# Two pieces to a step among the experts, later sparse transposes, and a branch hinted early, in a two-block model on one core

## Chip, cores and metric

The kernel runs on one core of one Trainium2 chip. The metric is the time of one execution in device microseconds, the median of several; a profiled execution gives the trace. The engines are called as the profile calls them: PE is TensorE's matmuls, PEld its weight loads, DVE VectorE, ACT ScalarE, POOL GpSimd and SP SyncE, which issues the DMAs. A "q" behind an engine's name is its sequencer. [...]

## What is computed

Everything is float32, for one sequence of 256 tokens of width 1024. A first block of two layers (neighbourhood attention and differential attention) comes first, then a second block of two layers: layer 0 mixes by native sparse attention (NSA), layer 1 by multi-head latent attention (MLA), each with a cross attention to a memory, and each is followed by a mixture of experts. That mixture is where most of the weights are: 16 experts with three matrices of 2 MB each.

```python
for i in range(DEPTH):                       # second block: NSA, then MLA
    ...
    y = jnp.concatenate([mix, xa], -1) @ w_out[i]
    x = layer_norm(DEEPNORM_ALPHA * x + y, ln_g[i, 0], ln_b[i, 0])
    f = hier_moe(x, ...)                     # 16 experts, 512 wide
    x = layer_norm(DEEPNORM_ALPHA * x + f, ln_g[i, 1], ln_b[i, 1])

# hier_moe, for the 256 tokens xs of the sequence: gate[s, e] is not zero for
# two experts of one group of four
hdn = jax.nn.silu(jnp.einsum('sd,edf->sef', xs, w_gate)) * jnp.einsum('sd,edf->sef', xs, w_up)
hdn = hdn * gate[..., None].astype(hdn.dtype)
return jnp.einsum('sef,efd->sd', hdn, w_down)
```

## The kernel before

The program is one stream of about 16,000 instructions. TensorE, VectorE and ScalarE execute what stands in their queues in the order in which the kernel's text issues it; within the experts and within NSA that order is written out by hand, in steps.

**Experts.** Each expert has room for 64 tokens (CAP). The tokens of a group of four experts are gathered by products with one-hot matrices `Dg` (`gather`, line 2025, 128 x 128 tiles), and the results are brought back by products with the transposed matrices `dT` (`combine`, line 2265). `back` (line 2051) makes `dT` and the gates. Between these, expert `e` has its own products, with tiles 64 columns wide, two of which run at once in the two halves of the array: gate and up (line 2173, tile `eg`), then down (line 2213, tile `dn`), which needs the hidden values: ScalarE's activation of the gate half (line 2180), VectorE's product (2183, 2193) and its transpose (2201, tile `hT`). The last expert's down products are done in quarters of the columns (line 2241), each followed by its sums (line 2514).

The function `moe` numbers the steps, 16 per expert, one pair of products in each second. `pre[s]` and `post[s]` are lists of what is issued before and behind step `s`, filled by `at`. `piece(s, gen, delay)` runs one piece of a generator (`gather`, `back` or `combine`) behind step `s` and its evacuation from PSUM `delay` steps later. So each piece is a run of full-array matmuls between 64-column ones. The rows of the norm's gain (`ln_row`, line 922) and the sums' first products (`begin` and `add`, lines 2465 and 2470) stand in the same lists.

**Weights.** `Weights` issues 192 DMAs of 512 KB per layer on SP's queue, in the order of use, into a ring of 12 slots "w" and into the tiles "b8" and "b4" that the rest of the kernel also uses. Which slots others need, and from which step to which, stands in the table `others`; a load is issued when a slot is free by it, and starts when the tile's last readers have finished.

**Overflow.** After the experts the count of tokens of the fullest expert is loaded into a register of each engine (line 2534). A conditional block (2535) computes what did not fit into 64 places, in a loop over the experts. With these inputs no expert has more than 64 tokens, so every engine jumps over the block. The last quarter's sums (line 2514) stand behind it.

**NSA.** Six pairs of heads go through a chain of steps: scores for two key halves (line 462), maxima (361), exponentials (370), normalisation on VectorE (1418, 1419 and 164, tile `z`), transposes of the second half for each head of the pair (1426) and of the first (1437), and the products with the values (1453, 1456). Pairs start four steps apart; between them TensorE has projections of NSA's other parts (line 253), whose weights VectorE and ScalarE split into two parts (lines 134 and 135).

## Time and profile before

| | us |
|---|---|
| median of 3 runs | 1029.16 |
| lowest, highest | 1028.06, 1031.38 |
| the profiled execution | 1031.01 |
| its span in the trace, first to last instruction | 1029.2 |
| PE busy in it | 992.5 (96%) |
| DVE busy | 658.8 (64%) |
| PEld busy | 647.2 (63%) |
| ACT busy | 440.0 (43%) |
| mean granted clock | 0.987 |

In that execution NSA's sparse attention stands at about 345 to 420, the experts of layer 0 from 461 to 680, MLA from 680 to 800 and the experts of layer 1 from 800 to 1020; a few us of norm and output end it. A busy share is a mean over stages that have different limits, so the prediction goes by stretches. Matmuls are pipelined: the duration of one in a row is longer than the distance to the next, and what a run of them costs is read from start to start.

### The profile page before, as it was taken

The page shows a single profiled execution, that of the slowest core. Times are in us where ns is not written, and L with a number is a line of the kernel's source. Part 1 is how long each engine was busy: PE and PEld are TensorE (multiplying, and loading weights), DVE is VectorE, ACT ScalarE, POOL GpSimd, SP SyncE. Part 2 cuts the span into 40 slices and gives each one's busy share as a digit, 9 for nine tenths or more (in the row PEclk, how much of TensorE's full clock was granted, in tenths as well). Part 3 has the DMA queues.
Part 4 walks back from the last instruction along what each step waited for, and adds up shares of the span by engine and source line. Part 5 has one row for each costly group of instructions (what it writes and reads, how often), then busy time and mean ns, then how long its engine had stood idle before and what let it go on. Part 6 is the DMA issues. An engine that isn't in the chain of part 4 may idle for free. (4 is left out here: it accounts for less than half of the span.)

```text
span 1029.2 us, 16197 instructions
## 1 busy us (share of the span) xinstructions
PE 992.5 (96%) x5673; PEld 647.2 (63%) x5673; DVE 658.8 (64%) x1852; ACT 440.0 (43%) x1094; POOL 19.0 (2%) x38
## 2 busy tenths in 40 slices
PE   8999999999999988999999999989999999999994
PEld 8898889978897766774333433368877443434332
DVE  6767876568877777748475545548885646454556
ACT  6556664556663567543212121134883321212121
POOL 1000000000100000000000000000000000000000
PEclk9999999999999999999999999989999999999998
DMA  8954665444666623889999999982698799999994
GB/s 298 374 152 144 203 197 184 144 127 119 184 197 214 174 87 121 292 344 327 355 409 409 409 409 409 393 309 87 206 349 320 256 332 410 375 409 409 409 406 149
DMA packets 110699, 285.64 MB, mean 278 GB/s; under 512 B 14160, under 2 KB 30864, under 8 KB 110352
## 3 DMA queue, kind: packets, MB, share of 16 engines
q1 hardware_dynamic: 110608, 284.50, 76.6%
q8 instruction: 49, 0.80, 0.3%
q14 instruction: 42, 0.34, 0.1%
HBM read 283.41 MB, written 1.05 MB: 276 GB/s over the span
## 5 line engine op out<-in xcount | busy, mean ns | idle before, releaser
L135 DVE TENSOR_TENSOR wsp<-w,wsp 128x512 fp32r<-128x512 f32 (+4 forms) x272 | 170.9, 643 | 66.3 <-ACT wsp L134 64.9
L2173 PE MATMUL eg<-wa,xg 128*64 128x512 f32 x776 | 208.7, 600 | 0.0
L253 PE MATMUL pj<-xTh,wsp 128*128 128x256 f32 x768 | 154.4, 291 | 1.1 <-ACT wsp L134 0.6
L134 ACT CAST wsp<-w 128x512 fp32r<-128x512 f32 (+4 forms) x272 | 148.5, 582 | 9.3 <-PE pj L253 8.7
L253 PEld LDWEIGHTS pj<-xTh,wsp 128*128 128x128 f32 x768 | 124.0, 192 | 8.1 <-issue 4.6
L2173 PEld LDWEIGHTS eg<-wa,xg 128*64 128x64 f32 x776 | 56.3, 136 | 89.2 <-issue 83.2
L253 PE MATMUL pj<-xTl,wsp 128*128 128x256 f32 x384 | 108.8, 283 | 0.0
L253 PE MATMUL pj<-wsp,xTh 128*128 128x512 f32 (+3 forms) x352 | 108.5, 389 | 0.0
L2183 DVE SCALAR_TENSOR_TENSOR z<-z,eg 64x512 f32<-64x512 f32 x32 | 21.7, 679 | 127.0 <-ACT z L2180 127.0
L2193 DVE SCALAR_TENSOR_TENSOR hq<-z,gall,eg 32x128 f32<-32x128 f32 x256 | 88.9, 347 | 4.4
L2213 PE MATMUL dn<-wa,hT 128*64 128x512 f32 x380 | 90.4, 592 | 0.0
L2173 PE MATMUL eg<-w,xg 128*64 128x512 f32 x248 | 83.5, 600 | 0.0
L253 PE MATMUL pj<-wsp,yTh 128*128 128x512 f32 x256 | 82.8, 404 | 0.0
L2180 ACT ACTIVATE z<-eg 64x512 f32<-64x512 f32 x32 | 18.9, 590 | 144.9 <-PE eg L2173 144.9
L2223 ACT CAST ys<-dn 64x512 fp32r<-64x512 f32 x60 | 34.8, 579 | 94.5 <-PE dn L2213 63.1
L253 PEld LDWEIGHTS pj<-xTl,wsp 128*128 128x128 f32 x384 | 73.7, 192 | 0.4
L253 PEld LDWEIGHTS pj<-wsp,xTh 128*128 128x128 f32 x352 | 62.8, 188 | 11.6 <-issue 2.5
L253 PE MATMUL pj<-wsp,xTl 128*128 128x512 f32 (+3 forms) x176 | 66.7, 379 | 0.0
L2213 PEld LDWEIGHTS dn<-wa,hT 128*64 128x64 f32 x380 | 27.3, 137 | 54.3 <-issue 51.4
L370 ACT ACTIVATE z<-z,mx 128x256 f32<-128x256 f32 (+1 forms) x104 | 48.1, 468 | 12.9 <-DVE mx L361 12.9
L253 PEld LDWEIGHTS pj<-wsp,yTh 128*128 128x128 f32 x256 | 45.8, 188 | 9.9 <-issue 1.9
L253 PE MATMUL pj<-wsp,yTl 128*128 128x512 f32 x128 | 50.2, 392 | 0.0
(418 smaller groups left out, 1458.0 us busy)
## 6 DMA issues: line engine op xcount, KB each, us to landing
wa<-moe_w_down_dram SPq DMA_DIRECT2D x100, 512.0 KB, 10.2
wa<-moe_w_up_dram SPq DMA_DIRECT2D x99, 512.0 KB, 10.1
wa<-moe_w_gate_dram SPq DMA_DIRECT2D x95, 512.0 KB, 9.3
w<-w_in_dram SPq DMA_DIRECT2D x64, 512.0 KB, 4.6
w<-moe_w_gate_dram SPq DMA_DIRECT2D x33, 512.0 KB, 10.1
w<-moe_w_up_dram SPq DMA_DIRECT2D x29, 512.0 KB, 9.9
w<-moe_w_down_dram SPq DMA_DIRECT2D x28, 512.0 KB, 10.2
w<-w_out_dram SPq DMA_DIRECT2D x24, 512.0 KB, 3.9
```

The source lines that it names most:

```text
L134: self.nc.scalar.copy(hi, src)
L135: self.nc.vector.tensor_sub(lo, src, hi)
L253: nc.tensor.matmul(o, a, b, start=begin and i == 0, stop=last and i == 2, skip_group_check=True)
L370: E.nc.scalar.activation(z[i], (src or z)[i], AF.Exp, bias=mx[:, i:i + 1], scale=1.0 if src else -1.0, accum_out=sm[:, i:i + 1])
L2173: self.E.nc.tensor.matmul(self.ps[b * CAP:b * CAP + CAP], self.xg[:, k, self.j], w, start=k == 0, stop=k == KD - 1, skip_group_check=True)
L2180: self.E.nc.scalar.activation(self.th, self.ps[:CAP], AF.Tanh, scale=0.5)
L2183: self.E.nc.vector.scalar_tensor_tensor(self.th, self.th, 1.0, self.ps[:CAP], op0=OP.add, op1=OP.mult)
L2193: self.E.nc.vector.scalar_tensor_tensor(self.hq[32 * q:32 * q + 32, :, h], th[:, q], self.gate()[r], u[:, q], op0=OP.mult, op1=OP.mult)
L2213: self.E.nc.tensor.matmul(self.pd[n * CAP:n * CAP + CAP], self.hT[:, k], self.w[2][k](0)[:, 512 * n:512 * n + 512], start=k == 0, stop=k == 3,
L2223: self.E.nc.scalar.copy(self.y[r, n], self.pd[r])
```

## The change

It has five parts.

- `piece` takes a number `m`, and runs that many pieces of a generator behind one step; their evacuations stand one step apart. Gathers come in three doubles in place of six (the planner's table keeps the matrix's slot six steps longer for it), combines in two in place of four, the rest of `back` in one in place of two.
- The gain's rows come two to a step (four products), the sums' first products two to a step, with their splits three steps apart instead of four.
- In NSA the second half's transposes of both heads of a pair are issued together behind step `s + 5` (before: behind `s + 4` and `s + 5`), and the steps behind them are one later.
- The count is loaded, and a hint for the branch is issued on PE, DVE and ACT, ahead of the last expert's quarters.
- The conditional block carries the label that the hint names.

```diff
-        for b, m in enumerate(ms):
-            flow.after(s + 4 + b, transpose1, m)
-            flow.before(s + 6 + b, transposed1, m)
-        flow.after(s + 6, transpose0, ms)
-        flow.before(s + 8, transposed0, ms)
-        flow.after(s + 9, values, ms)
-        flow.before(s + 11, lambda j=j: (E.split_to(yT[0], j, t["po", j]), E.free(t["po", j])))
+        for m in ms:
+            flow.after(s + 5, transpose1, m)
+            flow.before(s + 7, transposed1, m)
+        flow.after(s + 7, transpose0, ms)
+        flow.before(s + 9, transposed0, ms)
+        flow.after(s + 10, values, ms)
+        flow.before(s + 12, lambda j=j: (E.split_to(yT[0], j, t["po", j]), E.free(t["po", j])))
...
-            self.others["b4"] += [(s, 1), (s + 7, 1), (s + 19, 1), (s + 23, 1), (s + 24, -1), (s + 39, 1), (s + 55, 1)]
-            self.others["b4"] += [(s + 68, -1), (s + 69, -4)]
+            self.others["b4"] += [(s, 1), (s + 7, 1), (s + 19, 1), (s + 23, 1), (s + 30, -1), (s + 39, 1), (s + 55, 1)]
+            self.others["b4"] += [(s + 68, -5)]
...
-    def piece(s, gen, delay=2):
+    def piece(s, gen, delay=2, m=1):
 
         def run():
-            out = next(gen)
-            if delay:
-                at(pre, s + delay, out)
-            else:
-                out()
+            for k in range(m):
+                out = next(gen)
+                if delay:
+                    at(pre, s + delay + k, out)
+                else:
+                    out()
         at(post, s, run)
...
-            for d in (3, 5, 7, 13, 17, 20):
-                piece(s + d, it)
+
+            for d in (3, 9, 17):
+                piece(s + d, it, m=2)
...
-                for d, delay in ((41, 2), (45, 2), (51, 3), (50, 3)):
-                    piece(s + d, it, delay)
+                for d in (43, 50):
+                    piece(s + d, it, m=2)
...
-        for s in (10, 12):
-            piece(s, it)
+        piece(11, it, m=2)
...
-            at(post, 5 + 2 * m, lambda c=c, j=j: made.__setitem__(("ln", c, j), ln_row(E, i, 0, j, c)))
+            at(post, 5 + 4 * (m // 2), lambda c=c, j=j: made.__setitem__(("ln", c, j), ln_row(E, i, 0, j, c)))
...
-            at(pre, 16 * NE - 28 + 4 * k, lambda c=c, t=t: split(c, t))
-            at(post, 16 * NE - 26 + 4 * k, lambda c=c, t=t: begin(c, t))
+            at(pre, 16 * NE - 28 + 3 * k, lambda c=c, t=t: split(c, t))
+            at(post, 16 * NE - 24 + 6 * (k // 2), lambda c=c, t=t: begin(c, t))
...
+        if overflow:
+
+            most = nc.values_load(made["cnt"][0:1, 0:1], min_val=0, max_val=S)
+            tc.mark_branch_hint_location(f"overflow{i}", hint=most // (CAP + 1), engines=sorted(ENGINES, key=str))
...
-        most = nc.values_load(made["cnt"][0:1, 0:1], min_val=0, max_val=S)
-        with tc.If(most > CAP):
+        with tc.If(most > CAP, label=f"overflow{i}"):
```

What this does to TensorE's queue is seen at three places. The first is in the experts of layer 0, at a gather for the second group (line 2025), among gate and up products (`eg`, line 2173) and down products (`dn`, line 2213). Before:

```order
L2213 MATMUL dn<-wa,hT 64x512 x4
L2025 MATMUL xg<-Dg,xsh 128x256 x2
L2025 MATMUL xg<-Dg,xsl 128x256 x2
L2025 MATMUL xg<-Dg,xsh 128x256 x2
L2025 MATMUL xg<-Dg,xsl 128x256 x2
L2173 MATMUL eg<-wa,xg 64x512 x2
L2025 MATMUL xg<-Dg,xsh 128x256 x2
```

And now:

```order
L2213 MATMUL dn<-wa,hT 64x512 x4
L2025 MATMUL xg<-Dg,xsh 128x256 x2
L2025 MATMUL xg<-Dg,xsl 128x256 x2
L2025 MATMUL xg<-Dg,xsh 128x256 x2
L2025 MATMUL xg<-Dg,xsl 128x256 x2
L2025 MATMUL xg<-Dg,xsh 128x256 x2
L2025 MATMUL xg<-Dg,xsl 128x256 x2
L2025 MATMUL xg<-Dg,xsh 128x256 x2
L2025 MATMUL xg<-Dg,xsl 128x256 x2
L2173 MATMUL eg<-wa,xg 64x512 x6
```

Two pieces of eight matmuls have become one run of 16, and six products follow before the next.

The second place is the end of a layer on TensorE, with the last expert's quarters (`dn`, line 2241), the sums and the branch; line 2519 of the changed kernel is line 2514 of the one before.

```order
+L2510 TENSOR_LOAD cnt_i
+L2511 REGISTER_ALU
+L2717 BRANCH_PREFETCH_HINT
+L2241 MATMUL dn<-w,hT 64x256 x8
...
-L2514 MATMUL sum<-ys,dT 128x256 x4
-L2534 TENSOR_LOAD cnt_i
-L2535 COMPARE_AND_BRANCH
...
+L2519 MATMUL sum<-ys,dT 128x256 x4
+L2539 COMPARE_AND_BRANCH
```

The load of the count has moved from directly ahead of the branch to ahead of the quarters, and a hint stands there with it.

The third place is NSA on TensorE: a pair's scores (line 462), its transposes (`z`, line 1426), and projections in between.

```order
-L1426 MATMUL tp<-ident,z 128x128 x4
 L462 MATMUL sc<-KT,qT 128x512 x6
 L253 MATMUL pj<-xTh,wsp 128x256
...
 L1281 MATMUL tp<-ident,q 128x128 x2
-L1426 MATMUL tp<-ident,z 128x128 x4
+L1426 MATMUL tp<-ident,z 128x128 x8
```

The first head's four transposes have moved behind six scores and a block of projections, to where the second head's stood.

## Rows read from the trace of the kernel before

**Rows 1.** Windows of the experts; per engine busy us (instructions), then PEclk, DMA share, GB/s.

```profile
800.00:840.00 40.00, 40.00 (x197) 16.52 (x198) 25.95 (x66) 13.05 (x23) 0.00 (x0) 1.00 0.81 290
...
880.00:920.00 40.00, 40.00 (x192) 15.07 (x192) 18.93 (x46) 7.71 (x15) 0.00 (x0) 1.00 1.02 407
```

**Rows 2.** Timeline of TensorE, the ends of both layers of experts.

```profile
668.19 1.08 PE L2241 MATMUL dn<-wa,hT 128*64 128x256 f32 x8 [1.41 <-issue]
669.08 1.06 PE L2241 MATMUL dn<-w,hT 128*64 128x256 f32 x8
...
680.12 1.19 PE L2514 MATMUL sum<-ys,dT 128*128 128x256 f32 x4 [5.02 <-PEq L2535]
...
1018.16 0.71 PE L2514 MATMUL sum<-ys,dT 128*128 128x256 f32 x4 [2.83 <-PEq L2535]
```

**Rows 3.** Waits in NSA's attention, 347 to 412: us in total, times, longest.

```profile
PE tp L1426 <- DVE z L164: 8.6, 5, 3.4
```

**Rows 4.** Windows of NSA's attention and of the first us of MLA.

```profile
350.00:410.00 60.00, 51.45 (x377) 39.39 (x376) 47.79 (x235) 42.13 (x151) 0.31 (x1) 0.91 0.36 112
680.00:686.00 6.00, 5.88 (x24) 5.64 (x25) 3.68 (x10) 3.17 (x6) 0.70 (x1) 0.50 0.69 197
```

**Rows 5.** Timeline of all engines at one expert's end.

```profile
511.35 0.58 ACT L2223 CAST ys<-dn 64x512 fp32r<-64x512 f32 x1
...
511.61 0.45 DVE L2201 STREAM_TRANSPOSE hT<-hq 128x256 f32<-128x256 f32 x1
...
513.55 0.14 PEld L2213 LDWEIGHTS dn<-w,hT 128*64 128x64 f32 x2 [0.28 <-issue]
```

**Rows 6.** Timeline of TensorE, pieces of a gather between products.

```profile
484.50 1.08 PE L2173 MATMUL eg<-wa,xg 128*64 128x512 f32 x4
...
485.85 0.40 PE L2025 MATMUL xg<-Dg,xsl 128*128 128x256 f32 x2
486.09 0.40 PE L2025 MATMUL xg<-Dg,xsh 128*128 128x256 f32 x2
...
486.65 1.08 PE L2173 MATMUL eg<-wa,xg 128*64 128x512 f32 x4
```

**Rows 7.** Timeline of TensorE, a piece of a combine between products.

```profile
522.56 1.03 PE L2173 MATMUL eg<-wa,xg 128*64 128x512 f32 x4
523.52 1.19 PE L2265 MATMUL cb<-ys,dT 128*128 128x512 f32 x4
524.64 0.65 PE L2173 MATMUL eg<-wa,xg 128*64 128x512 f32 x2
```

**Rows 8.** Line 119, the last loads of layer 0: issue and landing.

```profile
L119 SPq DMA_DIRECT2D w<-moe_w_down_dram x1: 378/378/378, 653.0 to 653.0; - x1
...
DMA to landing us min/median/max: 11.6/11.6/11.6
```

**Rows 9.** Timeline of TensorE's weight loads, late in layer 1.

```profile
995.29 0.14 PEld L2173 LDWEIGHTS eg<-wa,xg 128*64 128x64 f32 x2 [0.28 <-issue]
995.72 0.14 PEld L2173 LDWEIGHTS eg<-wa,xg 128*64 128x64 f32 x2 [0.29 <-issue]
```

**Rows 10.** Line 2133, a late load of layer 1: issue and landing.

```profile
L2133 SPq DMA_DIRECT2D wa<-moe_w_up_dram x1: 328/328/328, 983.8 to 983.8; - x1
...
DMA to landing us min/median/max: 10.2/10.2/10.2
```

**Rows 11.** Line 2535, the branch, on the engines' sequencers (ns).

```profile
L2535 PEldq COMPARE_BRANCH  x2: 3661/4669/5677, 674.3 to 1014.3; - x2
...
L2535 DVEq COMPARE_BRANCH  x2: 56/64/72, 675.5 to 1015.5; - x2
```

**Rows 12.** Line 2534, the load of the count (ns).

```profile
L2534 PEldq TENSOR_LOAD <-cnt_i x2: 311/398/484, 673.7 to 1013.9; - x2
```

**Rows 13.** Timeline of VectorE, the last adds before the branch.

```profile
674.89 0.42 DVE L2251 TENSOR_TENSOR ys<-dn,ys 128x256 fp32r<-128x256 f32 x1 [0.58 <-ACT ys L2250]
...
1015.12 0.42 DVE L2251 TENSOR_TENSOR ys<-dn,ys 128x256 fp32r<-128x256 f32 x1 [0.59 <-ACT ys L2250]
```

## Prediction

> **What bounds the kernel now.** I read the page first: the totals, then the slices, then windows cut at the borders of the stages, then TensorE's timeline inside them. TensorE is busy in nearly all of the span, so the reader should look for two things only: stretches in which it does nothing, and stretches in which it is booked as busy and yet does less than it could.

> In the experts the windows show it busy without a break while the 16 DMA engines go from 0.81 of their time (800 to 840, 290 GB/s) to all of it (880 to 920, 407 GB/s) [rows 1]. Two limits thus lie close together: TensorE's own instructions, and a stream of 192 weight transfers of 512 KB per layer. At 407 GB/s one takes 1.29 us. Early in a layer the stream isn't full: it waits until TensorE has read a tile and given its slot back. Later it is full and can't be hurried.

> The idle stretches are few: 5.02 and 2.83 us at the end of each layer of experts, where the releaser is the branch of line 2535 [rows 2], and 8.6 us in five pieces in NSA's attention, before the transposes of line 1426, which wait for VectorE's scaled weights [rows 3].

> **Pieces two at a time.** A product with 64-column tiles is paired with another: weight loads of two instructions stand 0.43 us apart (995.29 and 995.72) [rows 9], 0.215 each. Gather matmuls inside a run are 0.12 apart (two from 485.85 to 486.09), yet four products and a run of eight gather matmuls, four rows of two, take 2.15 us from 484.50 to 486.65 [rows 6], where 4 x 0.215 + 8 x 0.12 = 1.82. So a change to full-array products and back costs 0.33. For the combine, four products and four of line 2265 take 2.08 (522.56 to 524.64) [rows 7], where eight times 0.215 is 1.72: 0.36. I take 0.35 for each interlude, whatever is in it. Counted over a whole layer in the order of TensorE's instructions, runs of full-array or 64-row products between 64-column ones fall from 41 to 25: ten fewer for gathers and combines, two for the norm's rows, two for the transposes of gates, two for the sums' begin. That is 16 x 0.35 = 5.6 us per layer, some four of the 16 before expert 4. No product is removed.

> The evacuations of both pieces move at most one step closer; their instructions stay. Their cover is the time between expert chain and use: for one expert the transpose on VectorE starts at 511.61, lasts 0.45 and is used at 513.55 [rows 5], a slack of 1.49, the smallest I found after expert 0; one evacuation on ScalarE is 0.58 [rows 5]. Two of them in the way fit. I cost this at nothing.

> **What the DMA lets through.** Once TensorE is faster, weights are late next. In layer 0 the tile of the last expert issued at 653.0 lands 11.6 later [rows 8], at 664.6, and its reader stands at 669.08 [rows 2]: 4.5 us of slack. In layer 1 one issued at 983.8 lands 10.2 later [rows 10], at 994.0, for a reader at 995.72 [rows 9]: 1.7 us. Added to it is what the stream itself comes earlier: until it is full it follows TensorE, and so gets the first four interludes, 1.4 us. Layer 0 may gain 5.9, so all 5.6 pass. Layer 1 may gain 1.7 + 1.4 = 3.1, and 2.5 of the 5.6 turn into waits on DMA. Bounds: 1.7 if the stream doesn't move, 5.6 if it moves with TensorE. The planner's table keeps one slot for a gathering matrix six steps longer; that it delays a load in the early part is the mechanism by which the stream would not move.

> **Count and hint early.** At the end of a layer TensorE's queue has a branch over the overflow loop, of 3.66 and 5.68 us, while VectorE's takes 0.06 [rows 11]. The branch is a long one for TensorE alone, which has the most code in the loop to jump over, so I read it as the fetch of what lies behind it. The change puts the count's load and the hint ahead of the last expert's quarters. After it, the four sums still wait for VectorE's last add, which begins at 674.89 and 1015.12 and takes 0.42 [rows 13]. Without the branch they could start at 675.4 and 1015.65 instead of 680.12 and 1018.16 [rows 2]: 4.7 and 2.5 us, 7.2 together. From the hint to the branch there are the quarters and the wait ahead of them: from 668.19 less 1.41 [rows 2] to the branch at 674.3 [rows 11], 7.5 us, against a longest stall of 5.68. The added work on TensorE's sequencer is a load of the count, 0.31 to 0.48 [rows 12]; it lies in the 1.41 us that TensorE stands still for the hidden values in front of its first quarter [rows 2]. If that cover were gone, it costs 0.5 per layer; VectorE's and ScalarE's loads are moved past nothing that anyone waits for longer.

> [...]

> **The clock behind the stall.** [...] At full clock 5.9 busy us would be 2.9 if nothing else bound it; copies by ScalarE stand between. I take 1.3, near half of that, with 0 and 2.9 as bounds. MLA's first weights are issued ahead of the branch on SP's queue, so none of them waits for what is shortened here.

> **Transposes later.** Both heads' transposes now start together, a step behind: where the second head's stood, which never waited. That removes the 8.6 us of waits [rows 3] if VectorE keeps up. But from 350 to 410 VectorE is busy 47.8 of 60 us and TensorE 51.5, at a clock of 0.91 [rows 4]: the stretch can't fall by more than 12.2. Upper bound 12 (all idle time and most of what the clock cost), lower 0: the change adds a wait as well, since the next pair's maxima want a tile that the transposes now read later; behind them on VectorE stand the splits of weights for line 253. Were the stretch 8.6 shorter, VectorE would be at 0.93. I take 5.5, nearer the row of waits than nothing, since part comes back as other waits.

> **The sum.** 5.5 + 5.6 + 4.7 + 1.3 + 3.1 + 2.5 = 22.7. The profiled execution took 1031.0, hence 1008.3; it stands 1.85 above the median of 1029.16, hence 1006.5 for a median.

> **The rivals.**
> *The hint fetches nothing* (or the early load is only an early load). For it: the program has no taken branch whose target was hinted, so no row shows one at work. Against it: it takes effect 8 us ahead. Then 4.7 + 2.5 + 1.3 stay: 1015.

> *VectorE keeps the attention where it is.* For it: 0.80 busy with chains of dependent small operations [rows 4]. Against: the second heads' transposes, one step later, found their values ready each time. Then 5.5 is lost: 1012.

> *The weight stream doesn't come earlier.* Layer 1 gains 1.7 and layer 0 4.5: 2.5 less, 1009.

> *Slower: bunched evacuations stand in front of the experts' hidden values.* Every expert's first down product waits for ScalarE's activation, VectorE's products and the transpose. Slack is 1.49 in the tightest [rows 5]. To eat 22.7 us and 3.1 more over 30 experts takes 0.86 us each, so a chain later by 2.35 even if all were as tight: four evacuations of 0.58 in the way each time. From 1.49 on it costs, from 2.35 on it decides: 1032 or more. The change moves two per piece, in some steps only, so this is unlikely.

> **How the numbers follow.** Under 0.3%, 3.1 us, this kernel's times can't tell a change from none. My forecast, 1006.5, has 0.55, with its own range of 1001 to 1012 from the bounds of attention, clock and stream. The hint failing has 0.16, VectorE holding 0.15, the stream 0.08, the slower case 0.04; 0.02 is left for several failing at once and no change. The range for all: below, attention at its upper bound gives 1000 and layer 1 uncapped 997.5, so 999; above, 1016 takes in each of the three rivals alone. Faster 0.92, same 0.04, slower 0.04.

> **What would show it.** Interludes: a gather run of 16 matmuls with one break of 0.35, and layer 0 shorter by some 5.6 between its first product and line 2241. Stream: waits on DMA of the weights before line 2173's loads, late in layer 1, where there are none now. Branch: the compare in TensorE's queue well under 1 us, line 2519's last sums within 0.3 us of VectorE's add, and the clock at 1.00 behind it. Attention: no wait of line 1426 over 1 us, and the stretch to line 417 shorter. I am wrong if the long compare is still there, if line 1426 waits elsewhere as long as before, or if down products begin to wait for VectorE.

## The result and the profile after

The median fell from 1028.61 to 1005.72 us (4 runs each, 1004.77 to 1006.84 after): a ratio of 0.9765, interval 0.9736 to 0.9795. The forecast was 1006.5. The profiled execution after is the quickest of its four (1004.77, span 1003.0) and the one before (1031.01, span 1029.2) lies 2.4 above its median, so differences between the two traces add up to 26.2 us where the medians differ by 22.9.

The first table cuts both executions at the same instructions of TensorE: the first product of the routing (line 1013), the first of the last expert's quarters (line 2241), the first transpose of the memory (line 159), and the same two in layer 1. The last stretch goes to the last busy instruction. All others are differences of starts in TensorE's timeline. An "interlude" is, as in the prediction, a run of full-array products between 64-column ones; a "piece" is one step's share of a gather or a combine.

| stretch, us | before | after | forecast | seen |
|---|---|---|---|---|
| start to routing 0, with NSA | 445.3 | 439.4 | -5.5 | -5.9 |
| experts, layer 0 | 222.9 | 217.8 | -5.6 | -5.1 |
| quarters and branch 0, MLA | 116.8 | 109.7 | -4.7 - 1.3 | -7.2 |
| experts, layer 1 | 223.4 | 217.8 | -3.1 | -5.6 |
| quarters, branch 1, end | 17.7 | 15.2 | -2.5 | -2.5 |

**Pieces.** TensorE's timeline at the same gather, as in [rows 6]:

```profile
476.82 0.50 PE L2025 MATMUL xg<-Dg,xsh 128*128 128x256 f32 x2
477.16 0.40 PE L2025 MATMUL xg<-Dg,xsl 128*128 128x256 f32 x2
...
478.59 0.40 PE L2025 MATMUL xg<-Dg,xsl 128*128 128x256 f32 x2
478.92 2.79 PE L2173 MATMUL eg<-wa,xg 128*64 128x512 f32 x12
481.64 0.51 PE L2025 MATMUL xg<-Dg,xsh 128*128 128x256 f32 x2
```

The sixteen gather matmuls begin at 476.82 and the next product at 478.92: 2.10 us where 16 x 0.12 is 1.92. The twelve products behind them take 2.72 where 12 x 0.215 is 2.58. So a run has one break of 0.3, as each piece had before. The 5.1 us of layer 0 hold a wait of 0.81 at line 2466, where 0.07 was before (VectorE's splits come late there); without it 5.8, over 16 interludes, is 0.36 each. In layer 1 the wait is 0.81 instead of 0.61, and 5.6 becomes 5.8 as well.

**Weights.** The weight loads of the tile of [rows 9, 10] in layer 1, and its issue and landing:

```profile
972.02 0.14 PEld L2173 LDWEIGHTS eg<-wa,xg 128*64 128x64 f32 x2 [0.29 <-issue]
```

```profile
L2133 SPq DMA_DIRECT2D wa<-moe_w_up_dram x1: 327/327/327, 960.8 to 960.8; - x1
...
DMA to landing us min/median/max: 10.2/10.2/10.2
```

It lands at 971.0 and is used at 972.02: 1.0 us of slack, where 1.7 was left before, although its use comes 5.6 us earlier in the layer. The stream came 4.9 earlier, not 1.4. But this tile is not the tightest. The last down tile of the last expert but one lands at 982.24, and its weight load has to wait for it:

```profile
982.28 0.20 PEld L2213 LDWEIGHTS dn<-wa,hT 128*64 128x64 f32 x4 [0.70 <-DMA wa<-moe_w_down_dram]
```

Its neighbours stand 0.29 idle, so 0.4 of the 0.70 is the wait. It costs nothing yet, since the next product (line 2241) waits 1.4 us for its hidden values in any case. Before, this tile landed at 1004.26 for a reader at 1005.56, 1.3 us of slack. In layer 0 the like tile had 3.7 (661.64 for 665.33) and now 0.04 (654.50 for 654.54). So both layers now stand at what the weights allow.

The windows and the waits of SP's queue say where the stream of layer 1 gained: the 10 us before from 870 to 880 have a DMA share of 0.88 at 330 GB/s, and the answering window after is full. In the first, SP waits 6.0 us to issue a load of line 119, because the first combine's last products (line 2265) still have to read the slot; after, 1.4. First the two windows, then the two waits, before and after each time:

```profile
870.00:880.00 10.00, 10.00 (x50) 4.61 (x46) 9.67 (x17) 2.92 (x5) 0.00 (x0) 1.00 0.88 330
...
847.00:857.00 10.00, 10.00 (x50) 4.99 (x49) 9.45 (x17) 1.86 (x4) 0.00 (x0) 1.00 1.02 408
...
SPq L119 <- PE cb L2265: 6.0, 1, 6.0
...
SPq L119 <- PE cb L2265: 1.4, 1, 1.4
```

That slot comes back 85.3 us into the layer instead of 91.9, 6.6 earlier, while TensorE's own lead there is 2.0 to 2.7 us (first products of the experts around it). A combine in two doubles ends earlier by more than TensorE does.

**Branch.** The compare of [rows 11], and TensorE's timeline at the end of layer 0, as in [rows 2]:

```profile
L2539 PEldq COMPARE_BRANCH  x2: 440/544/647, 662.8 to 990.2; - x2
...
L2539 DVEq COMPARE_BRANCH  x2: 68/76/84, 664.0 to 991.5; - x2
```

```profile
657.27 1.95 PE L2241 MATMUL dn<-w,hT 128*64 128x256 f32 x16 [1.42 <-DVE hT L2201]
...
663.44 1.63 PE L2519 MATMUL sum<-ys,dT 128*128 128x256 f32 x8
664.90 1.37 PE L159 MATMUL tp<-ident,mem 128*128 128x128 f32 x11
666.62 0.60 PE L159 MATMUL tp<-ident,mem 128*128 128x128 f32 x4 [0.35 <-issue]
```

The compare is 0.65 in layer 0 and 0.44 in layer 1, in place of 5.68 and 3.66. The last sums follow at once, MLA's transposes begin at 664.90, and there is one more stop of 0.35 for which the trace names no other engine. Of the 7.2 us of this stretch, 5.3 lie ahead of MLA's first transpose and 1.9 behind it. The windows of [rows 4], NSA's attention and the first us of MLA:

```profile
350.00:410.00 60.00, 53.17 (x416) 41.19 (x414) 52.79 (x253) 44.83 (x160) 0.31 (x1) 1.00 0.46 140
667.00:673.00 6.00, 6.00 (x32) 5.31 (x31) 1.61 (x3) 2.35 (x4) 0.56 (x1) 1.00 0.96 350
```

MLA starts at a granted clock of 1.00, the profile's full speed, without a slow stretch. In the attention TensorE has 53.2 busy us of 60 instead of 51.5, VectorE 52.8 instead of 47.8. Its waits, to be held against [rows 3]:

```profile
PE tp L1426 <- DVE z L164: 3.2, 3, 2.6
...
PE tp L1426 <- DVE qT L1286: 1.4, 1, 1.4
PE sc L462 <- DVE mx L361: 1.1, 2, 1.0
PE po L1453 <- DVE mx L361: 1.1, 1, 1.1
```

Line 1426 still waits for 4.6 us, and 2.2 us of waits have moved to the scores and the values.

### The profile page after: what moved, and what is told of

It reads as the page before. It is cut to its first block, busy times and chain, and to the rows that moved or that the text cites. A ratio compares the mean times of both kernels' runs of the same rounds, so it can differ in the third digit from the quotient of the medians.

```text
span 1003.0 us, 16229 instructions
## 1 busy us (share of the span) xinstructions
PE 973.8 (97%) x5673; PEld 644.8 (64%) x5673; DVE 656.4 (65%) x1852; ACT 439.0 (44%) x1094; POOL 19.1 (2%) x38
## 5 line engine op out<-in xcount | busy, mean ns | idle before, releaser
L2173 PE MATMUL eg<-wa,xg 128*64 128x512 f32 x784 | 201.3, 596 | 0.0
L2213 PE MATMUL dn<-wa,hT 128*64 128x512 f32 x372 | 88.2, 592 | 0.0
L2173 PE MATMUL eg<-w,xg 128*64 128x512 f32 x240 | 76.2, 598 | 0.0
L253 PEld LDWEIGHTS pj<-wsp,xTh 128*128 128x128 f32 x352 | 62.8, 188 | 11.6 <-issue 2.5
L2213 PEld LDWEIGHTS dn<-wa,hT 128*64 128x64 f32 x372 | 26.6, 137 | 53.2 <-issue 48.2
## 6 DMA issues: line engine op xcount, KB each, us to landing
wa<-moe_w_up_dram SPq DMA_DIRECT2D x100, 512.0 KB, 10.1
wa<-moe_w_down_dram SPq DMA_DIRECT2D x97, 512.0 KB, 10.2
wa<-moe_w_gate_dram SPq DMA_DIRECT2D x96, 512.0 KB, 10.1
w<-moe_w_gate_dram SPq DMA_DIRECT2D x32, 512.0 KB, 10.2
w<-moe_w_down_dram SPq DMA_DIRECT2D x31, 512.0 KB, 10.2
```

Of the source, the lines that this page charges most:

```text
L253: nc.tensor.matmul(o, a, b, start=begin and i == 0, stop=last and i == 2, skip_group_check=True)
L2173: self.E.nc.tensor.matmul(self.ps[b * CAP:b * CAP + CAP], self.xg[:, k, self.j], w, start=k == 0, stop=k == KD - 1, skip_group_check=True)
L2213: self.E.nc.tensor.matmul(self.pd[n * CAP:n * CAP + CAP], self.hT[:, k], self.w[2][k](0)[:, 512 * n:512 * n + 512], start=k == 0, stop=k == 3,
```

## Experiments

The kernel before ran beside each on the same chip; its medians there were 1029.2 to 1031.2, so the ratios to it are what is compared. The changed kernel has 0.9765.

| run | what | median us | ratio, interval |
|---|---|---|---|
| e12 | before, with count and hint | 1023.15 | 0.9936, 0.9918 to 0.9954 |
| e13 | before, with pieces; count loaded early | 1022.66 | 0.9924, 0.9895 to 0.9952 |
| e4 | before, with the table | 1028.95 | 0.9995, 0.9976 to 1.0014 |
| e1 | changed, no hint | 1017.22 | 0.9880, 0.9856 to 0.9903 |
| e2 | changed, old NSA | 1015.01 | 0.9843, 0.9808 to 0.9879 |
| e3 | changed, old pieces | 1021.27 | 0.9920, 0.9898 to 0.9943 |
| e8 | changed, combines single | 1007.76 | 0.9789, 0.9756 to 0.9823 |
| e6 | changed, combines in one; part of the output left out | 1009.17 | 0.9790, 0.9770 to 0.9809 |
| e7 | changed, NSA a step later | 1011.76 | 0.9808, 0.9788 to 0.9827 |
| e9 | changed, hint 18 us earlier | 1006.60 | 0.9758, 0.9739 to 0.9777 |
| e11 | e9 with old NSA | 1012.48 | 0.9838, 0.9807 to 0.9870 |
| e10 | changed, no hint, 80 small products ahead of the branch | 1041.80 | one execution |

### Without the hint

```diff
-            tc.mark_branch_hint_location(f"overflow{i}", hint=most // (CAP + 1), engines=sorted(ENGINES, key=str))
...
```

> The changed kernel without the hint; the count is still loaded early. If the stall at the branch is a fetch that only the hint starts, the compare in TensorE's queue takes some 4 to 6 us again in both layers, the clock falls behind the first one, and the time is 1005.7 + 7.2 + 2.5 = 1015.4 us (the two differences that the traces show from line 2241 to MLA's routing and from line 2241 to the end). Rival: the long compare was a wait for the count's load, which now comes early; then the time stays at 1005.7.

The time is 11.5 above the changed kernel's, 12 by the ratios. The hint it is, not the early load. The compare is 3.43 in layer 0, less than expected, and 6.55 in layer 1. First the compare (the branch is line 2538 here), then TensorE's timeline behind the branch of layer 0:

```profile
L2538 PEldq COMPARE_BRANCH  x2: 3431/4992/6554, 665.0 to 999.0; - x2
...
668.61 0.71 PE L2518 MATMUL sum<-ys,dT 128*128 128x256 f32 x4 [2.18 <-PEq L2538]
669.16 1.47 PE L159 MATMUL tp<-ident,mem 128*128 128x128 f32 x12
673.85 0.85 PE L159 MATMUL tp<-ident,mem 128*128 128x128 f32 x4 [3.21 <-DVE x L1584]
```

After the branch (2.18) it stops again, 3.21 us, after twelve transposes. The row names VectorE's `x` as releaser; but the changed kernel, with the same code there, went on at 666.62, before its own `x` was begun (667.68). So the name is a coincidence of time. What fits is a second block of instructions: a DMA view of the half us from 671.5 on has one packet on the instruction queue, and TensorE moves 2.3 us after it. The changed kernel's stop of 0.35 has such a packet too, at 664.15, 2.5 ahead of the next row. In each of nine profiles with a stop at this place, of 0.2 to 3.2 us, the row behind it begins 2.2 to 2.8 us after such a packet.

### Old transposes, old pieces

```diff
-            flow.after(s + 5, transpose1, m)
+            flow.after(s + 4 + b, transpose1, m)
...
```

> The changed kernel with NSA's transposes where they were before. If the later transposes are what shortened the attention, its waits before line 1426 are 8 to 9 us in total again and the time is 1005.7 + 5.9 = 1011.6 us, 5.9 being what the routing product after NSA comes earlier by. Rival, VectorE sets the attention's length and the 5.9 came from elsewhere: within 1 us of 1005.7.

The attention was right, its old waits came back (8.2 us). But 9.3 us were lost (8.0 by the ratios), not 5.9. The four times go from 1009.6 to 1017.7, and the profile is that of the last. In it, the branch's compare, with its hint, and the DMA queues from 671 to 672 (packets, MB, share):

```profile
L2539 PEldq COMPARE_BRANCH  x2: 1267/2734/4202, 670.4 to 1001.7; - x2
```

```profile
q1 hardware_dynamic: 202, 0.39, 105.2%
q8 instruction: 1, 0.02, 6.8%
```

A compare of 4.2 us in layer 0 and 1.27 in layer 1. The hint of layer 0 was issued at 662.4, and the instruction packet starts at 672.0, among weights at 406 GB/s: 9.6 us, where the changed kernel's took 5.6, from 655.3 to 660.9. The changed kernel's DMA queues from 660 to 661:

```profile
q1 hardware_dynamic: 130, 0.38, 99.5%
q8 instruction: 1, 0.02, 6.8%
```

```diff
-            for d in (3, 9, 17):
-                piece(s + d, it, m=2)
+            for d in (3, 5, 7, 13, 17, 20):
+                piece(s + d, it)
...
-                for d in (43, 50):
-                    piece(s + d, it, m=2)
+                for d, delay in ((41, 2), (45, 2), (51, 3), (50, 3)):
+                    piece(s + d, it, delay)
...
```

> The changed kernel with all pieces, norm rows, sums' begins and the planner's table as before; NSA and the hint stay. By the interludes alone (0.35 each, 16 per layer) 11.2 us go: 1016.9. By the cap that the prediction put on layer 1 (3.1 there, 5.6 in layer 0) 8.7: 1014.4. By the two traces (5.1 and 5.6) 10.6: 1016.3.

The experts gave back 5.1 and 5.6, as in the two traces; yet the time went up by 15.6, more than any of the three sums. Of the rest, 1.6 lies ahead of the routing, where the clock fell in the attention (one of the three falls to 0.50 told of below), and 4.3 in MLA, in TensorE's timeline and in windows behind the branch:

```profile
671.58 1.47 PE L159 MATMUL tp<-ident,mem 128*128 128x128 f32 x12
676.04 0.84 PE L159 MATMUL tp<-ident,mem 128*128 128x128 f32 x4 [2.99 <-DVE x L1584]
```

```profile
669.70:673.70 4.00, 3.20 (x26) 2.51 (x23) 2.66 (x10) 1.86 (x4) 0.16 (x1) 1.00 0.96 336
675.70:679.70 4.00, 3.66 (x12) 3.03 (x12) 0.60 (x2) 2.36 (x4) 0.00 (x0) 0.57 1.06 379
```

The hinted block is there (a compare of 0.39), the second isn't: a stop of 2.99 with the DMA engines at 0.96, the packet at 673.8, the clock then at 0.57. MLA took 106.3 us instead of 102.0. In layer 1 the hinted block itself was late, with a compare of 1.82.

### The hint earlier

```diff
+        def early_hint():
+            most = made["most"] = nc.values_load(made["cnt"][0:1, 0:1], min_val=0, max_val=S)
+            tc.mark_branch_hint_location(f"overflow{i}", hint=most // (CAP + 1), engines=sorted(ENGINES, key=str))
+            at(post, 16 * NE - 16, early_hint)
...
```

> The changed kernel with the count's load and the hint a further 15 steps earlier, some 22 us ahead of the branch. If the hinted block is only sometimes there because its transfer stands behind the weights on the DMA engines (6 to 9 us), more lead makes it safe: TensorE's compare under 0.2 us in both layers and a time of 1004 to 1006 us. Rival: the sequencer keeps a hinted block only until its own code needs the place; then the stalls are back and the time is near that without a hint, 1017.

TensorE's compare of this run:

```profile
L2541 PEldq COMPARE_BRANCH  x2: 355/381/407, 664.1 to 993.1; - x2
```

The hint stands 25.6 us ahead of the branch of layer 0 here, instead of 7.5, and the hinted block stays: 0.4 in both layers. The median is the changed kernel's, and the interval lies over its own: no gain where the old lead was enough. Its trace shows what the profile of the changed kernel hid, the clock behind the attention's longest wait (2.6 us at 387). The window:

```profile
380.00:400.00 20.00, 17.39 (x118) 13.64 (x118) 15.40 (x77) 16.29 (x60) 0.00 (x0) 0.83 0.25 80
```

Here the clock was 0.83 as a mean from 380 to 400; in the changed kernel's profile it stayed at 1.00. From the first row of line 1281 to the routing this took 122.4 us against 120.6, and 126.9 before. The seven profiles with these transposes all have that wait; behind it the clock fell to 0.50 in three of them, for 3.4 to 6.8 us (121.7 to 122.4 for the stretch), and not in the other four (120.6). With the old transposes, in six profiles, the clock fell two or three times each, and the stretch took 125.4 to 126.9.

> The changed kernel with NSA's old transposes, as in the run that had a compare of 4.2 us in spite of the hint, and with the hint 15 steps earlier. If that compare was a hinted block still on its way, it falls under 0.5 us in both layers and 3 to 4 of the 1015.0 us go: 1011 to 1012, NSA's 5 to 6 us alone being left against 1005.7. If the lead is not what was short, 1015 again.

The compare fell to 0.40 and 0.35: lead was what was short there. That the time fell with it is not shown: 0.9838 and 0.9843 are the same ratio within their intervals, and this profile has a second stop of 1.71 us.

### Is a fetch short when nothing else is in flight?

```diff
-            tc.mark_branch_hint_location(f"overflow{i}", hint=most // (CAP + 1), engines=sorted(ENGINES, key=str))
...
-        E.warm(0)
+        E.warm(80)
...
```

> The changed kernel without the hint and with 80 small products on TensorE in front of the branch, which feed nothing: they delay the branch by about 9 us, until in layer 1 no weights are in flight. If the fetch itself is short and waits behind other transfers, TensorE's compare in layer 1 falls from 6.6 us to under 1.5, while in layer 0, where SP goes on with MLA's weights, it stays over 2. Rival, a fetch costs the same 3 to 6 us whatever else is in flight: 5 us or more in layer 1 again. The time, with twice 9 us added, says nothing.

The compare of this run, and the window in which it stands in layer 1 (the last number is GB/s):

```profile
L2538 PEldq COMPARE_BRANCH  x2: 3321/3334/3347, 679.5 to 1025.4; - x2
```

```profile
1025.00:1029.00 4.00, 2.66 (x25) 2.50 (x24) 0.00 (x0) 0.00 (x0) 0.00 (x0) 1.00 0.01 4
```

The theory failed in half: at 4 GB/s the compare in layer 1 is still 3.3 us. Layer 0, where nothing moved at the branch either, has 3.35. The instruction packets divide this time. "Idle" is a DMA share of at most 0.2 from the compare's start to the packet, "busy" one of 0.67 or more:

| compare without a hint | DMA engines | begins | packet starts | ends |
|---|---|---|---|---|
| this run, layer 1 | idle | 1025.42 | 1026.38 | 1028.74 |
| before, layer 1 | idle | 1014.34 | 1015.36 | 1018.00 |
| before, layer 0 | busy | 674.28 | 677.44 | 679.96 |
| pieces alone, layer 0 | busy | 669.04 | 672.16 | 674.65 |
| pieces alone, layer 1 | busy | 1003.00 | 1006.95 | 1009.54 |
| no hint, layer 1 | busy | 999.02 | 1003.03 | 1005.57 |

In all ten such compares, 1.0 to 1.1 us pass before the packet where the engines are idle and 2.6 to 4.0 where they are busy, and 2.3 to 2.7 behind its start. So a fetch took 3.3 to 3.7 here with idle engines, and what else is in flight came on top. That need not be weights: in layer 1 of the run without the hint their last tile had landed at 996.0. In flight were the rows of the last norm (line 169), issued 0.9 us ahead of the compare; in the kernel before they had landed by 1013.0, ahead of its compare. The issue of the first in the run without the hint:

```profile
L169 SPq DMA_DIRECT2D lngb<-ln_g_dram x1: 351/351/351, 998.1 to 998.1; - x1
```

### The hint alone, the pieces alone

> The kernel before with the early count and hint alone. Were the branch's share of the change free of the others, 7.2 + 2.5 = 9.7 us would go: 1019. If TensorE must also fetch the block behind the hinted one, and that transfer again stands behind MLA's weights (as in the run with single pieces, where TensorE stood 3.0 us among line 159's transposes), only about 5 go: 1024.

> The kernel before with the pieces in doubles, the norm rows, the sums' begins and the planner's table alone. By the traces 5.1 + 5.6 = 10.7 us go in the experts: 1018.5, if the two branch stalls cost what they did before. Where the layer ends with the weights closer behind it, the stalls may each be up to 2 us longer: 1022.

The hint alone gave 6.6 by the ratio, between the two theories. The compare of layer 0 was still 1.40, TensorE stopped for 0.89 behind the branch, and the profiled stretches were 9.1 shorter (the profile before lies 2.4 above its median). The pieces alone shortened the experts by 5.1 and 5.6 in the trace, yet the time by 7.8: the compare was 5.6 and 6.5 instead of 5.7 and 3.7, and the last stretch 20.7 instead of 17.7. In layer 1 the instruction packet starts 3.95 us into the compare instead of 1.0 (the table above), which fits the rows of the norm in front of it.

### What paces the experts

```diff
-            self.others["b4"] += [(s, 1), (s + 7, 1), (s + 19, 1), (s + 23, 1), (s + 24, -1), (s + 39, 1), (s + 55, 1)]
+            self.others["b4"] += [(s, 1), (s + 7, 1), (s + 19, 1), (s + 23, 1), (s + 30, -1), (s + 39, 1), (s + 55, 1)]
...
```

> The kernel before with the planner's new table alone; TensorE's order is untouched. It asks why the weights of layer 1 came 4.9 us earlier than the layer itself. If the table does it, the load that is read last but few in layer 1 (expert 15's up, second part) has 4 to 6 us of slack in place of 1.8 and the DMA share from 870 to 880 is near 1.0 instead of 0.88, with the time still within 1.5 us of 1028.6, since TensorE paces the layer there. If TensorE's earlier reads do it, the slack stays at 1.8 and the time at 1028.6. Should the table itself carry part of the gain, the time is 2 us or more lower.

The same tile as above is issued at 983.8, lands 10.2 later and is used here (the weight loads), and the window from 870 to 880 is as it was:

```profile
995.79 0.14 PEld L2173 LDWEIGHTS eg<-wa,xg 128*64 128x64 f32 x2 [0.29 <-issue]
```

```profile
870.00:880.00 10.00, 10.00 (x50) 4.77 (x48) 9.67 (x17) 2.68 (x5) 0.00 (x0) 1.00 0.91 345
```

Slack 1.8, share 0.91, and SP's wait for the combine is 6.0 us as before. The table alone did nothing.

```diff
-                for d in (43, 50):
-                    piece(s + d, it, m=2)
+                for d in (43, 45, 50, 52):
+                    piece(s + d, it)
```

> The changed kernel with the combines' four pieces one to a step (behind 43, 45, 50 and 52) in place of two doubles: six interludes more in each layer. At 0.35 each the stretch from the routing to line 2241 grows by 2.1 in both layers, 217.8 to 219.9, and the time by 4.2 to about 1010. If the weights were what paced the layers, TensorE's extra time would hide and it would stay near 1005.7.

Six was a miscount: two of the new runs touch a gather's, so it is four more. The time rose by 2.0 (2.5 by the ratios), not by 4.2. Layer 0 took 218.8 and its wait at line 2466 fell from 0.81 to 0.29: 1.45 for four interludes, 0.36 each. Layer 1 took 219.3, because there the weights are late, as SP's wait and a weight load show:

```profile
SPq L119 <- PE cb L2265: 6.9, 1, 6.9
...
986.21 0.20 PEld L2213 LDWEIGHTS dn<-wa,hT 128*64 128x64 f32 x4 [1.09 <-DMA wa<-moe_w_down_dram]
```

The tile of [rows 10] lands 2.4 us earlier in the layer than before, where the changed kernel has 4.9. So about half of the stream's gain is that it follows TensorE; the other half is the slot that a combine in two doubles gives back early.

```diff
-                for d in (43, 50):
-                    piece(s + d, it, m=2)
+                piece(s + 50, it, m=4)
```

> The changed kernel with each combine's four pieces in one run in place of two: three interludes fewer in each layer. If TensorE still paces the experts, 6 x 0.35 = 2.1 us less, 1003.6. If the weights do (in layer 0 and at layer 1's end they land 0.04 us before their use), at most 0.5 us less and longer waits on DMA in front of line 2213.

In this run the split for the first of the sums stands ahead of the add of the last combine's first part, which leaves that part out of the output. It was no faster (0.9790 against 0.9765), with 218.8 and 219.5 in the experts where the changed kernel has 217.8. Part is a longer wait for the splits (1.41 instead of 0.81); another part is here, in a weight load of layer 0 and the tile's issue and landing:

```profile
623.36 0.19 PEld L2173 LDWEIGHTS eg<-w,xg 128*64 128x64 f32 x2 [1.02 <-DMA w<-moe_w_up_dram]
```

```profile
L2133 SPq DMA_DIRECT2D w<-moe_w_up_dram x1: 327/327/327, 613.2 to 613.2; - x1
...
DMA to landing us min/median/max: 10.1/10.1/10.1
```

Issued at 613.2, landed 10.1 later at 623.3, used at 623.36: TensorE waits for weights, and three interludes fewer in each layer bring nothing.

### One step later still

```diff
-            flow.after(s + 5, transpose1, m)
+            flow.after(s + 6, transpose1, m)
...
```

> The changed kernel with NSA's transposes and all behind them one step later still. If what is left of the waits in the attention (6.6 us, the longest 2.60 for VectorE's scaled weights at 387) is only lateness of those weights, 2 to 3 us go: 1003. If VectorE's work as a whole sets the pace, nothing is gained, and the longer chain at the end may cost up to 3: 1005.7 to 1009.

Slower by 4.4 against the changed kernel by the ratios, more than the 3 that were allowed for. Line 1426 waits no more; these do, in NSA's attention:

```profile
PE sc L462 <- DVE mx L361: 2.4, 3, 1.7
...
PE sc L462 <- ACT pT L1430: 1.6, 2, 1.4
...
PE tp L159 <- DVE xq L1290: 0.9, 1, 0.9
...
PE pj L253 <- DVE qT L1286: 0.8, 1, 0.8
```

TensorE's waits come to 6.3 us in place of 6.8: they have moved to others, most of them for VectorE. And the chain behind line 1925 is 3.6 us longer (33.6 to the routing in place of 30.0). The clock also fell to 0.50 for 6.8 us from 387 on, as in the run with the early hint, so not all of the 4.4 is the step's doing. That VectorE paces the attention fits this and is not shown by itself: it was busy 52.8 of 60 us.

## Why the prediction was right, point by point

- **Interludes** (0.35 forecast): 0.36 from the traces of both layers, 0.36 in the run with single combines. Right, place and price.
- **The cap on layer 1** (3.1 of 5.6): the term that was mis-sized. The mechanism is there, as the run with single combines shows (a wait for weights of 1.09 late in layer 1), and the changed kernel has just reached it (0.4). The step that failed is "it gets the first four interludes, 1.4 us". I read a full stream from windows of 40 us; cut to 10, the one at 870 has room (330 GB/s). The stream gained 4.9: 2.4 by following TensorE longer, as with single combines, and by difference 2.5 from the slot of the first combine, which the sum did not have. The slack of 1.7 was not the smallest either (1.3 in layer 1; 3.7, not 4.5, in layer 0).
- **Branch and clock** (4.7 + 2.5 + 1.3): 7.2 + 2.5 seen. The first rival is out: with the hint the compares are 0.65 and 0.44 us, without it 3.43 and 6.55. But "7.5 us against a longest stall of 5.68" left the wrong margin: from a hint to its packet 3.5 to 9.6 us passed (14 cases, DMA share 0.52 to 1.08), and 2.3 to 2.8 more until a compare that waited for it was over. The block was in time in the changed kernel's profile, and late, with compares of 1.3 to 4.2, with NSA's old order (both layers), with old pieces (layer 1), with the hint alone, with combines in one and with NSA a step later (layer 0). So that it was in time is partly luck. And the sum knew only one block; the stop that reads as a second one takes up to 3.2 (3.21 without the hint). The 1.3 for the clock, taken from [rows 4] with 0.50 as half speed, is an estimate that no run shows by itself: seen are 1.9 of the 7.2 us behind MLA's first transpose, with a clock of 1.00 from 667 to 673.
- **Attention** (5.5, between 0 and 12): 5.9 in the profile, 4.5 where the clock fell; 3.0 to 6.4 over all profiles. "No wait of line 1426 over 1 us" was wrong, 2.6 and 1.4 are left. VectorE's pace was the reason given for taking half, and moving the transposes once more fits it.
- **Slower by evacuations**: the compare of stages gives nothing for it; both layers took 217.8 to 218.6 in every run with these pieces.
- **The sum as a sum**: between the profiles, for which it was made, the terms come to 26.2, not 22.7; 2.5 of the difference is layer 1's cap and 1.2 the branch with MLA. That the medians differ by 22.9 is luck in part.
- **Parts don't add.** By the ratios the pieces gave 7.8 alone (2.9 either way, from the intervals) and 16.0 (3.8) beside the other two; the hint 6.6 alone (1.9) and 11.8 (3.9) beside the others; the attention 1.6 (3.0) beside the hint, 4.5 (3.8) beside the pieces and 8.0 (4.7) beside both. Only the pieces differ far beyond these bounds: without the hint they lost 2.9 at layer 1's branch, and without them the second block cost 3.0 in MLA. The attention alone was not run.

What is not settled: why SP sends MLA's weights so much earlier in some runs that the second block stands behind them, how much of the time from a hint to its packet is a queue and how much something else, and what the 2.2 to 2.8 us between an instruction packet and TensorE's next row are.

No run beat the changed kernel by more than its interval; that with the early hint is as quick.

## What to carry to other kernels

Cut a window to a few transfers' length before calling a stream full, and read what the issuing queue waits for: a mean of 0.98 over 40 us (840 to 880) hid a wait of 6.0 us for one slot. Give a hint for a branch the lead that its instruction packet takes with transfers in flight, here up to 9.6 us and 2.8 behind it, not the stall that it removes, 5.68 at most before; and look for a second such stop behind the branch, here of up to 3.2 us. Where two parts of a change end in one place, time them together and each undone, since what one gains the other's stall may eat.

## What the hardware showed that I had not expected

```profile
q8 instruction: 49, 0.80, 0.3%
```

That is 0.80 MB in 49 packets. In the ten compares without a hint the packet began 1.0 to 1.1 us into the compare where the DMA engines were idle and 2.6 to 4.0 where they were busy, and the compare ended 2.3 to 2.7 us behind that; at idle engines it took 3.3 to 3.7 in all. With the early hint it took 0.36 and 0.41.
